# Sums and differences of the MLP token quarters: issued on VectorE instead of GpSimd

## The chip, the cores and the metric

The kernel runs on one core of one Trainium2 chip. The metric is the device time of one execution in microseconds, as the median of several runs. A core has TensorE (PE in the profile, with its weight loads as PEld), VectorE (DVE), ScalarE (ACT), GpSimd (POOL) and a queue that mostly starts DMA transfers (SP). Each takes its instructions in the order in which the built program lists them; they meet through semaphores.

## The reference

One decoder layer on 2048 tokens of width 1024, in float32: a mixing block (retention beside a pooling mixer), a cross-attention into 256 memory tokens, and a gated MLP, each with a root-mean-square norm before it and a residual add behind it. The change touches the MLP alone:

```python
def conv_glu_ffn(h, w_up, conv_w, conv_b, w_down):
    a = h @ w_up
    ...
    c = conv_w[0] * a2 + conv_w[1] * a1 + conv_w[2] * a + conv_b
    gate, val = jnp.split(c, 2, axis=-1)
    return (jax.nn.silu(gate) * val) @ w_down
```

`w_up` is 1024 x 5632 and `w_down` 2816 x 1024; `a1` and `a2` are `a` shifted by one and two tokens.

## The kernel before

Tokens stand along the free axis, in two blocks of 1024 (`b` = 0 and 1) with two halves of 512. A float32 matmul is made of three passes over high and low parts (`passes`, lines 241 to 243), so every operand is first split: ScalarE copies the high part, and VectorE subtracts it to get the low part.

The MLP multiplies with seven products in place of eight (a Strassen scheme). The tokens' matrix and the weights are both seen as 2 x 2 quarters, and each product takes one sum or difference of quarters from each side. The weights' sums are made earlier by DMA (`weight_sums`, lines 918 to 925). The tokens' sums are the subject here. `sums_of` (line 964) takes four 128 x 512 quarters and makes four results in a chain: `t = b22 - b12`, `b12 = b11 - b12`, then `b11 = b11 + t`, `b21 = b11 - b21`. Three of them are written over the quarters. It is called in two places:

- `normed_tiles` makes the inputs of the up projection. For each of four pairs of feature tiles, four quarters come from the DRAM buffer `Xd`, are scaled by the norm (VectorE, line 225, `T<-T,vecs`), three are stored to `Hd`, then come the sums, and four sums are stored to `Hd`. Block 0 does this beside the cross-attention (`first_tiles`), block 1 beside the up projection of block 0 (`later_tiles`). That makes 8 calls.
- `pair` inside `Up.conv` makes the inputs of the down projection. When the gated product of a second feature tile of a pair is done (line 216, `Z<-Z`, 128 x 1024), its two halves are stored to `Gd`, two quarters of the first tile are loaded back from `Gd` into `T`, and the sums follow; they too are stored to `Gd`. With 11 pairs in each of two blocks that makes 22 calls.

So there are 30 calls, with 120 instructions of 128 x 512. The last of the four writes over a quarter that is being stored to `Gd` or `Hd`, and has to wait until that store has been read out.

`combining` loads one sum from `Hd` or `Gd` (line 949), splits it (ScalarE line 956, VectorE line 216 `G<-T,G`), and the result is the right-hand operand of a product. `Member.fetch` loads weights (line 1001), `high` and `low` split them (ScalarE line 1007, VectorE `Q<-R,Q` and `G<-R,G`). `evac` adds or copies a finished product from a PSUM bank into the gate or value tile (VectorE `Z<-Z,mm`). `conv` then runs three taps (ScalarE line 1070, VectorE line 225 `Z<-Z,vecs` of 128 x 1024, twice), SiLU (ScalarE line 1082) and the gated product. GpSimd copies the two tokens at a block's edge into and out of `halo` (lines 1067 and 1069) in `one`.

There are five PSUM banks named `mm`, seven places for split weight pairs and a handful of 128 x 512 temporaries (`T`, and pieces of `consts` and `state`).

The order on each engine is not the order of the source: the kernel is built with `schedule_with_timeline_sim=True`, so that a scheduler orders each engine's instructions by its own estimate of when they can run. Data dependences and buffers are those of the source.

Of the kernel before, what the change touches and what calls it, by code (L numbers as in the profile page):

```python
# [12 lines left out]
ALU = mybir.AluOpType  # L13
# [106 lines left out]
def trunk(ctx, tc, xT, memT, pos, w_qkgu, w_v, wkv, wqT, wo, wout_r, wout_p, poolT, w_up, w_dn, vecs, consts, outT):  # L120
    nc = tc.nc
    pe, act, dve, pool, sp = nc.tensor, nc.scalar, nc.vector, nc.gpsimd, nc.sync
# [64 lines left out]
    t = TT.take()  # L187
# [27 lines left out]
    def tt(eng, out, a, b, op):  # L215
        return eng.tensor_tensor(out=out, in0=a, in1=b, op=op)  # L216
# [746 lines left out]

    def sums_of(b11, b12, b21, b22, t):

        tt(pool, t, b22, b12, ALU.subtract)
        tt(pool, b12, b11, b12, ALU.subtract)
        yield
        tt(pool, b11, b11, t, ALU.add)
        tt(pool, b21, b11, b21, ALU.subtract)  # L970
        yield

    def send(to, aps):
# [53 lines left out]
    class Up(Member):  # L1027
# [29 lines left out]
        def conv(self, g):  # L1057
# [26 lines left out]
            def five():  # L1084
# [15 lines left out]
                def pair():  # L1100
                    if TT.room() < 3:
                        after(1, pair)
                        return
                    x = [TT.take() for _ in range(3)]
                    b11, b12, t = (r.f[:, :SUB] for r in x)
                    sp.dma_start(b12, to[7])
                    sp.dma_start(b11, to[0])
                    todo = sums_of(b11, b12, one, two, t)

                    def keep():  # L1110
                        send(to, {4: t, 1: b12, 2: b11, 6: one})
                        for r in (*x, c):
                            r.free()

                    after(2, lambda: next(todo))
                    after(3, lambda: next(todo))
                    after(5, keep)
# [311 lines left out]
    def normed_tiles(b, j, q, rb):  # L1429

        for i, v in enumerate(q):
            n, s = j + 4 * (i // 2), i % 2
            stt(v, v, ffng[:, n : n + 1], rb[s].f[:, :SUB], ALU.mult, ALU.mult)
        if j == KT // 2 - 1:
            for r in rb:
                r.free()
        yield
        send(Hd[b, j], {0: q[0], 5: q[3], 3: q[2]})
        t = TT.take()
        todo = sums_of(*q, t.f[:, :SUB])  # L1440
        next(todo)
        yield
        next(todo)
        yield
        send(Hd[b, j], {4: t.f[:, :SUB], 1: q[1], 2: q[0], 6: q[2]})
        t.free()
        yield
# [281 lines left out]
```

## Time and profile before

| | |
|---|---|
| median of 3 runs | 2493.02 us (2491.94 to 2494.43) |
| the profiled execution | 2497.84 us |
| its span, first to last instruction | 2495.7 us, mean granted TensorE clock 0.991 |
| PE busy | 2441.3 us (98%), 11390 instructions |
| DVE busy | 1704.0 us (68%), 2789 instructions |
| ACT busy | 1220.2 us (49%), 2171 instructions |
| POOL busy | 374.2 us (15%), 364 instructions |

A row of the timeline or of the groups names the engine, the line, the operation, "output tiles<-input tiles" with buffer numbers left out, and the shape. "[1.2 <-X]" is idle time of that engine ahead of the instruction and what ended it. PEclk is the share of full speed that TensorE was granted. The MLP's part of the span runs from about 1060 us, where block 0's inputs are made beside the cross-attention, to the end.

### The profile page before, as it was taken

What the parts mean: (1) busy time and instruction counts of PE and PEld (TensorE: products, weight loads), DVE (VectorE), ACT (ScalarE), POOL (GpSimd) and SP (SyncE); (2) the same over time, 40 slices, a digit from 0 to 9 for tenths busy, and PEclk for the clock granted to TensorE, in tenths of its full rate; (3) what the DMA queues carried; (4) which work ended last, traced back from release to release, by engine and by line L of the source; (5) the groups of instructions that cost most, each with busy time, mean ns of one, the idle gap of its engine ahead of it and who ended that gap; (6) DMA issues with size and microseconds to landing.
All of it is one profiled execution on the core that took longest, in us unless ns stands there. A gap on an engine that the chain in (4) does not pass through costs nothing. (4 is left out here: it accounts for less than half of the span.)

```text
span 2495.7 us, 33069 instructions
## 1 busy us (share of the span) xinstructions
PE 2441.3 (98%) x11390; PEld 2039.3 (82%) x11390; DVE 1704.0 (68%) x2789; ACT 1220.2 (49%) x2171; POOL 374.2 (15%) x364
## 2 busy tenths in 40 slices
PE   6999999999999999999998999999999999999997
PEld 6888788888788888888887888888888887888885
DVE  8646576564636574575777776896677687877875
ACT  6333423443321223434654555675555576666663
POOL 1010111100111110030025130332113021000001
PEclk9999999999999999999999999999999999999998
DMA  9363889716766764365567565665556468768951
GB/s 317 91 169 110 232 193 244 230 46 208 223 136 151 153 160 152 101 247 199 175 203 250 182 195 158 206 225 172 157 164 214 132 217 300 244 190 282 340 166 68
DMA packets 257176, 474.27 MB, mean 190 GB/s; under 512 B 26864, under 2 KB 56176, under 8 KB 257008
## 3 DMA queue, kind: packets, MB, share of 16 engines
q1 hardware_dynamic: 212336, 408.18, 49.7%
q0 software_dynamic: 19584, 34.61, 9.1%
q10 hardware_dynamic: 25088, 29.37, 3.4%
q8 instruction: 89, 1.46, 0.2%
q14 instruction: 79, 0.65, 0.1%
HBM read 370.87 MB, written 170.39 MB: 217 GB/s over the span
## 5 line engine op out<-in xcount | busy, mean ns | idle before, releaser
L241 PE MATMUL mm<-G,Q 128*128 128x512 f32 (+1 forms) x1888 | 728.3, 386 | 16.1 <-ACT Q L233 10.5
L243 PE MATMUL mm<-G,Q 128*128 128x512 f32 (+1 forms) x1888 | 727.1, 386 | 4.5 <-DVE Q L216 4.5
L242 PE MATMUL mm<-G,Q 128*128 128x512 f32 (+1 forms) x1888 | 726.2, 385 | 0.0
L241 PE MATMUL mm<-G 128*128 128x512 f32 (+1 forms) x1380 | 531.5, 387 | 10.4 <-DVE Z L216 7.3
L243 PE MATMUL mm<-G 128*128 128x512 f32 (+1 forms) x1380 | 532.8, 387 | 2.3 <-DVE G L216 2.3
L242 PE MATMUL mm<-G 128*128 128x512 f32 (+1 forms) x1380 | 533.0, 386 | 0.0
L241 PEld LDWEIGHTS mm<-G,Q 128*128 128x128 f32 x1888 | 358.2, 190 | 84.2 <-ACT Q L233 11.2
L243 PEld LDWEIGHTS mm<-G,Q 128*128 128x128 f32 x1888 | 357.7, 190 | 73.6 <-DVE Q L216 5.4
L242 PEld LDWEIGHTS mm<-G,Q 128*128 128x128 f32 x1888 | 358.3, 190 | 68.0 <-DVE G L216 0.4
L241 PEld LDWEIGHTS mm<-G 128*128 128x128 f32 x1380 | 260.4, 189 | 64.6 <-DVE Z L216 6.3
L243 PEld LDWEIGHTS mm<-G 128*128 128x128 f32 x1380 | 260.6, 189 | 54.6 <-DVE G L216 2.8
L242 PEld LDWEIGHTS mm<-G 128*128 128x128 f32 x1380 | 260.8, 189 | 51.6
L225 DVE SCALAR_TENSOR_TENSOR Z<-Z,vecs 128x1024 f32<-128x1024 f32 x176 | 244.8, 1394 | 55.4 <-ACT Z L1070 50.7
L216 DVE TENSOR_TENSOR Q<-R,Q 128x512 fp32r<-128x512 f32 x235 | 176.0, 751 | 152.2 <-ACT Q L233 142.5
L1007 ACT ACTIVATE G<-R 128x512 fp32r<-128x512 f32 (+1 forms) x272 | 167.1, 615 | 228.7 <-PE mm L242 222.0
L216 DVE TENSOR_TENSOR G<-R,G 128x512 fp32r<-128x512 f32 (+1 forms) x268 | 197.0, 743 | 114.4 <-ACT G L1007 76.0
L216 DVE TENSOR_TENSOR Z<-Z,mm 128x512 f32<-128x512 f32 x284 | 193.6, 682 | 89.3 <-PE mm L243 88.9
L233 ACT ACTIVATE Q<-R 128x512 fp32r<-128x512 f32 x150 | 93.6, 628 | 246.2 <-PE mm L242 219.1
L216 DVE TENSOR_TENSOR G<-T,G 128x512 fp32r<-128x512 f32 (+1 forms) x201 | 135.0, 686 | 51.9 <-ACT G L956 38.4
L1007 ACT ACTIVATE Q<-R 128x512 fp32r<-128x512 f32 (+1 forms) x204 | 125.2, 614 | 76.3 <-PE mm L242 61.9
L1070 ACT ACTIVATE Z<-Z,vecs 128x1024 f32<-128x1024 f32 x88 | 109.3, 1242 | 52.4 <-DVE Z L216 50.8
L941 ACT ACTIVATE aux<-R 128x512 f32<-128x512 f32 (+1 forms) x184 | 105.4, 575 | 47.8 <-DVE Q L216 23.8
(217 smaller groups left out, 2647.7 us busy)
## 6 DMA issues: line engine op xcount, KB each, us to landing
R<-Ud SPq DMA_DIRECT2D x176, 256.0 KB, 2.8
T<-Gd SPq DMA_DIRECT2D x168, 256.0 KB, 4.2
R<-w_up SPq DMA_DIRECT2D x132, 256.0 KB, 3.1
Gd<-Z SPq DMA_DIRECT2D x110, 256.0 KB, 2.5
Ud<-w_up SPq DMA_DIRECT2D x88, 256.0 KB, 6.2
R<-w_qkgu SPq DMA_DIRECT2D x32, 512.0 KB, 4.5
R<-Dd SPq DMA_DIRECT2D x64, 256.0 KB, 4.2
Gd<-T SPq DMA_DIRECT2D x56, 256.0 KB, 3.1
```

Of the source, the lines that this page charges most:

```text
L216: return eng.tensor_tensor(out=out, in0=a, in1=b, op=op)
L225: dve.scalar_tensor_tensor(out=out, in0=a, scalar=s, in1=b, op0=op0, op1=op1)
L233: act.activation(hi, src, AF.Copy)
L241: pe.matmul(ps, lh, rh, start=start, stop=False, skip_group_check=more)
L242: pe.matmul(ps, lh, rl, start=False, stop=False, skip_group_check=more)
L243: pe.matmul(ps, ll, rh, start=False, stop=stop, skip_group_check=more)
L941: act.activation(t, x, AF.Copy)
L1007: act.activation(p2[:, 0, :w], self.raw[i].f[:, :w], AF.Copy)
L1070: act.activation(self.c[g].f, a[:, 2:], AF.Identity, bias=cb[:, f : f + 1], scale=cw[2][:, f : f + 1])
```

## The change

VectorE issues the four instructions of `sums_of`, in both places from which it is called. Nothing else in the source differs; the copies of the block edges and seven multiplications near the end stay on GpSimd.

```diff
     def sums_of(b11, b12, b21, b22, t):
 
-        tt(pool, t, b22, b12, ALU.subtract)
-        tt(pool, b12, b11, b12, ALU.subtract)
-        yield
-        tt(pool, b11, b11, t, ALU.add)
-        tt(pool, b21, b11, b21, ALU.subtract)
+        tt(dve, t, b22, b12, ALU.subtract)
+        tt(dve, b12, b11, b12, ALU.subtract)
+        yield
+        tt(dve, b11, b11, t, ALU.add)
+        tt(dve, b21, b11, b21, ALU.subtract)
         yield
```

Since a scheduler sets the order, the built program differs in more than these 120 instructions. The order of the engines is the same up to the last part of block 1's cross-attention and again in the last part of the down projection; between them PE, VectorE, ScalarE and the SP queue have rows in another order.

## The prediction

> **What bounds the kernel now.** I read the page's first part, then the busy times by stage, PE's waits, the stretches where PE stood, and there the timelines. The span first; the sum is made against the profiled execution of 2497.84 us, 2.1 us more than its span and 4.8 us (0.2%) above the median of the runs, 2493.02. I take the difference from the profile and subtract it from the median.
>
> ```profile
> span 2495.7 us, 33069 instructions
> ```
>
> The busy times by stretch:
>
> ```profile
> core 0: us, PE busy (x) PEld busy (x) DVE busy (x) ACT busy (x) POOL busy (x), PEclk, DMA share, GB/s
> 1626.00:1655.00 29.00, 28.74 (x127) 23.43 (x126) 29.00 (x34) 23.51 (x39) 14.59 (x11) 1.00 0.63 212
> 2045.00:2068.00 23.00, 23.00 (x104) 19.03 (x103) 23.00 (x25) 17.63 (x31) 8.56 (x6) 1.00 0.61 196
> 1352.00:1372.00 20.00, 13.37 (x45) 9.68 (x44) 18.68 (x17) 7.79 (x12) 14.36 (x10) 0.74 0.80 273
> 2070.00:2080.00 10.00, 7.87 (x28) 6.00 (x27) 5.72 (x11) 5.48 (x11) 1.44 (x2) 0.83 1.01 360
> 1376.00:1396.00 20.00, 20.00 (x89) 16.54 (x89) 16.80 (x21) 11.53 (x17) 2.07 (x3) 1.00 0.62 192
> ```
>
> The last row is PE at its pace: 89 matmuls in 20 us, 0.225 us each. TensorE bounds the kernel, and another engine matters only where PE stands. Where the moved instructions run, I find two such places. In 1352 to 1372 there were 45 matmuls, so 44 x 0.225 = 9.9 us were lost, part of it to a clock of 0.74 in these 20 us. In 2070 to 2080 there were 28 where 44.5 fit: 16.5 x 0.225 = 3.7 us. Together 13.6 us, which is all that the change can give back. PE's waits in 1280 to 1420, then in 2030 to 2085, name VectorE both times:
>
> ```profile
> PE mm L241 <- DVE Z L216: 5.2, 2, 4.2
> PE mm L243 <- DVE G L216: 2.3, 1, 2.3
> ```
> ```profile
> PE mm L241 <- DVE Z L216: 2.1, 1, 2.1
> ```
>
> **What the change takes from GpSimd.** Line 216's instructions from 1060 to 2080 us, by engine:
>
> ```profile
> core 0: us, DVE busy (x) POOL busy (x), PEclk, DMA share, GB/s
> 1060.00:2080.00 1020.00, 468.10 (x641) 199.03 (x120) 0.99 0.60 196
> ```
>
> The 120 on POOL are the sums: 199.03 us, 1.66 each. GpSimd bounds nothing, so this by itself is worth nothing. What counts is what they do to VectorE meanwhile. The groups of VectorE from 1200 to 2160 us, which hold 26 of the 30 calls:
>
> ```profile
> L225 DVE SCALAR_TENSOR_TENSOR Z<-Z,vecs 128x1024 f32<-128x1024 f32 x176 | 244.8, 1394 | 55.4 <-ACT Z L1070 50.7 <-issue 2.8 <-DMA R<-Ud 1.1
> L216 DVE TENSOR_TENSOR G<-R,G 128x512 fp32r<-128x512 f32 x142 | 113.4, 799 | 78.0 <-ACT G L1007 75.0 <-DMA Gd<-Z 3.0
> L216 DVE TENSOR_TENSOR Z<-Z,mm 128x512 f32<-128x512 f32 x155 | 105.5, 681 | 25.5 <-PE mm L243 25.2
> L216 DVE TENSOR_TENSOR Q<-R,Q 128x512 fp32r<-128x512 f32 x81 | 67.0, 827 | 8.9 <-ACT Q L1007 8.9
> ```
>
> and the same groups from 1500 to 1585 us, where no sum runs:
>
> ```profile
> L225 DVE SCALAR_TENSOR_TENSOR Z<-Z,vecs 128x1024 f32<-128x1024 f32 x18 | 23.1, 1281 | 7.6 <-ACT Z L1070 7.6
> L216 DVE TENSOR_TENSOR Z<-Z,mm 128x512 f32<-128x512 f32 x14 | 9.6, 683 | 2.0 <-PE mm L243 1.8
> L216 DVE TENSOR_TENSOR G<-R,G 128x512 fp32r<-128x512 f32 x13 | 9.0, 689 | 16.3 <-ACT G L1007 13.3 <-DMA Gd<-Z 3.0
> L216 DVE TENSOR_TENSOR Q<-R,Q 128x512 fp32r<-128x512 f32 x9 | 6.2, 686 | 1.6 <-ACT Q L1007 1.6
> ```
>
> The three groups that read both operands from SBUF are slower in the first table; the one that reads PSUM (`Z<-Z,mm`) is not (681 against 683 ns). So VectorE loses time while GpSimd makes sums: 176 x 0.113 = 19.9 us, 142 x 0.110 = 15.6, 81 x 0.141 = 11.4, together 46.9 us, or 1.8 us for each of 26 calls.
>
> **What it adds to VectorE.** 120 instructions of 128 x 512 with both inputs in SBUF. The timeline of VectorE around the first stall gives their price, and the stall's course:
>
> ```profile
> 1346.52 0.75 DVE L225 SCALAR_TENSOR_TENSOR T<-T,vecs 128x512 f32<-128x512 f32 x1 [5.73 <-DMA T<-Xd]
> ...
> 1349.92 0.75 DVE L225 SCALAR_TENSOR_TENSOR T<-T,vecs 128x512 f32<-128x512 f32 x1 [2.05 <-DMA T<-Xd]
> 1350.59 1.28 DVE L225 SCALAR_TENSOR_TENSOR Z<-Z,vecs 128x1024 f32<-128x1024 f32 x1
> 1351.78 1.78 DVE L216 TENSOR_TENSOR Q<-R,Q 128x512 fp32r<-128x512 f32 x1
> 1353.49 0.68 DVE L216 TENSOR_TENSOR Z<-Z,mm 128x512 f32<-128x512 f32 x1
> 1354.08 1.71 DVE L225 SCALAR_TENSOR_TENSOR Z<-Z,vecs 128x1024 f32<-128x1024 f32 x1
> 1355.72 1.57 DVE L216 TENSOR_TENSOR G<-R,G 128x512 fp32r<-128x512 f32 x1
> 1357.21 2.31 DVE L216 TENSOR_TENSOR Z<-Z 128x1024 f32<-128x1024 f32 x1
> ...
> 1361.43 1.97 DVE L225 SCALAR_TENSOR_TENSOR Z<-Z,vecs 128x1024 f32<-128x1024 f32 x1 [0.23 <-ACT Z L1070]
> 1363.33 0.67 DVE L216 TENSOR_TENSOR Z<-Z,mm 128x512 f32<-128x512 f32 x1
> ```
>
> The instruction at 1353.49 is 0.68 us long, and the next starts 0.59 later: such an instruction holds the engine for 0.60 us. 120 x 0.60 = 72 us in all, 2.4 us for a call. Against the 1.8 us won back, VectorE's load grows by 0.6 us a call, 18 us in 1000 (the smaller groups, which I did not count, would lower this). That is no load that a stage could feel.
>
> The Trainium skill's page "VectorE: DVE Perf Modes", section "The DRAIN you can't avoid", speaks against the change: there the next VectorE instruction does not start until the pipeline is empty. By that rule a sum costs its whole 0.68 us, 82 us in all. The rows with starts 0.59 apart contradict it for instructions that do not depend on each other; inside a call the third and fourth do depend, so the truth may lie between.
>
> **The first stall, 9.9 us.** VectorE stood 5.73 and then 2.05 us for transfers `T<-Xd`, and got behind. From 1349.92 it then worked through its list slowly, since GpSimd ran sums beside it: `Q<-R,Q` took 1.78 in place of 0.69, `G<-R,G` 1.57 in place of 0.69, two `Z<-Z,vecs` 1.71 and 1.97 in place of 1.28: 3.1 us in these four alone. PE waited until the addition `Z<-Z,mm` at 1363.33 was over (1364.0). The transfers were late because the queue that starts them stood for sums on GpSimd; its timeline (one merged row for three stores of sums, 4.72 us, and the load behind them):
>
> ```profile
> 1337.22 4.72 SPq L975 DMA_DIRECT2D Gd<-T  x3
> ...
> 1342.52 0.40 SPq L1453 DMA_DIRECT2D T<-Xd  x1
> ```
>
> A call lasts 4 x 1.66 = 6.6 us on GpSimd and some 2.4 us, plus what is put between, on VectorE, so these stores, and the loads behind them, come earlier. In the changed kernel's order, between the last of the two scalings at 1349.92 and that `Z<-Z,mm` stand one product addition, one `G<-R,G` and two sums: 0.67 + 4 x 0.60 + 0.68 = 3.75 us, done at 1353.7 in place of 1364.0 even if the transfer lands no earlier. I take the whole 9.9 us as gone. If the cover fails (the sums wait there too), 3.1 us remains as the gain.
>
> **The second stall, 3.7 us.** ScalarE, then VectorE:
>
> ```profile
> 2071.81 0.63 ACT L956 ACTIVATE G<-T 128x512 fp32r<-128x512 f32 x1 [7.34 <-DMA T<-Gd]
> ```
> ```profile
> 2072.47 0.69 DVE L216 TENSOR_TENSOR G<-T,G 128x512 fp32r<-128x512 f32 x1 [3.77 <-ACT G L956]
> 2073.08 0.68 DVE L216 TENSOR_TENSOR Z<-Z,mm 128x512 f32<-128x512 f32 x1
> ```
>
> VectorE waited for a late load of a sum, and the addition that PE needed was queued behind. In the changed order that addition stands ahead of these `G<-T,G`. But PE needs the late operand too, soon after. Between 0 and 3.7 I take half, 1.9.
>
> **The new wait.** The fourth instruction of a call overwrites a quarter that is being stored. The page's row for that store:
>
> ```profile
> Gd<-Z SPq DMA_DIRECT2D x110, 256.0 KB, 2.5
> ```
>
> On GpSimd nobody stood behind this wait but the copies of the block edges; on VectorE the additions that free PE's banks do, and the low parts of weights. The closest place in the new order has two other instructions and three sums between the gated product and the fourth: 5 x 0.60 = 3.0 us against 2.5 and the issue, so a wait of some tenths. The bounds for all calls: nothing, or one stall like the first, 9.9. I take 2, since most gaps are wider. The edge copies, no longer queued behind 6.6 us of sums, cost nothing and can only come earlier. The 16 sums beside the cross-attention add 9.6 us to VectorE there; no PE wait on VectorE is seen in it, five PSUM banks cover it, and I take nothing (at most 9.6).
>
> **Sum:** -9.9 - 1.9 + 2 = -9.8 us. Profiled execution 2497.84 - 9.8 = 2488.0; median 2493.02 - 9.8 = 2483.2, so 2483. What a measurement of this kernel can tell from no change is about 0.2%, 5 us: faster is below 2488, slower above 2498.
>
> **Rivals.** *The transfers alone made the stalls.* For it: 5.73 + 2.05 us of standing ahead of the first one, and a load ahead of the second; and VectorE's load does not shrink. Then only the 3.1 us are won, 2490: no change that can be told. Against it: the new order has less between load and addition.
>
> *VectorE, waiting in order, starves PE.* Place: 1626 to 1655 and 2045 to 2068, where the table shows VectorE busy without a gap and two calls close together. Eight sums and two waits for stores, 8 x 0.60 + 2 x 2.5 = 9.8 us, could stand ahead of the additions. The first stall shows from where it decides: PE stood after VectorE had stood 7.8 us and lost 3.1, 10.9 in all. If it happens once, at the price of the seen stall, and the old ones stay: 2493 + 9.9 = 2503. Against it: GpSimd's sums take 1.8 us a call from VectorE in these places now, and PE lost next to nothing in them.
>
> *The change doesn't do what it says:* excluded, the built program has 120 more instructions on VectorE and 120 fewer on GpSimd.
>
> **Chances.** Forecast, both stalls mostly gone: 0.55. No change: 0.18. Slower: 0.27; the schedule between 1060 and 2170 us is a new one, and any wait in it lands on an engine that was hardly ever late. The range: at the lower end all 13.6 us, 2479, and a microsecond for the runs' spread, 2478; at the upper end 2500, which leaves out the worse half of the slower case.
>
> **What would show it.** Right: POOL busy near 175 us; `G<-R,G` and `Q<-R,Q` at 0.69 throughout; PE's waits on VectorE in 1280 to 1420 under 2 us and no slice with a low PEclk there. Wrong: a new PE wait on `Z L216` or `G L216` with VectorE standing ahead of it for a DMA into or out of `Gd`, `Hd` or `Xd`; or `T<-T` on VectorE well over 0.7 us.

## The result, and the profile after

The changed kernel takes 2477.96 us (median of 6 runs, 2475.03 to 2482.13) where the kernel before took 2493.01 on the same chip (6 runs, 2490.11 to 2495.33). The ratio is 0.9944, with a 95% interval of 0.9934 to 0.9954: 15.05 us or 0.6% faster. Its profiled execution took 2477.89 us.

The page of the changed kernel, its span, its busy times and the store that the fourth sum of a call waits for:

```profile
span 2476.1 us, 33012 instructions
...
PE 2434.1 (98%) x11390; PEld 2034.9 (82%) x11390; DVE 1707.3 (69%) x2909; ACT 1219.5 (49%) x2171; POOL 187.3 (8%) x244
...
Gd<-Z SPq DMA_DIRECT2D x110, 256.0 KB, 2.7
```

VectorE executes 120 instructions more and is busy only 3.3 us longer (1704.0 before). Where the 15 us were lost is counted best in matmuls. These are the busy times by stretches of 100 us of the kernel before, in the columns that the prediction's table has:

```profile
1300.00:1400.00 100.00, 92.41 (x392) 74.88 (x391) 78.95 (x85) 49.44 (x75) 45.36 (x31) 0.95 0.73 244
1600.00:1700.00 100.00, 99.74 (x440) 82.28 (x439) 87.44 (x104) 69.15 (x113) 33.45 (x25) 1.00 0.69 226
2000.00:2100.00 100.00, 97.87 (x425) 80.57 (x424) 82.10 (x107) 71.83 (x134) 28.52 (x19) 0.98 0.76 253
```

and of the changed kernel:

```profile
1300.00:1400.00 100.00, 100.00 (x443) 82.81 (x442) 85.98 (x115) 54.00 (x83) 9.32 (x11) 1.00 0.75 251
1600.00:1700.00 100.00, 100.00 (x443) 82.81 (x442) 83.32 (x108) 64.73 (x99) 16.17 (x16) 1.00 0.59 197
2000.00:2100.00 100.00, 99.67 (x440) 82.19 (x439) 85.12 (x133) 76.89 (x145) 0.19 (x1) 1.00 0.85 286
```

PE at its pace makes 443 in 100 us, so one takes 0.2257 us. The three stretches hold 51, 3 and 15 matmuls more: 11.5, 0.7 and 3.4 us, together 15.6, about the 15.05 between the medians. (The two profiled executions lie 19.6 us apart in span. The other 4 us lie ahead of 1100 us, mostly in 200 to 300 us, where the order of the engines is the same in both kernels and the profiled execution before, 4.8 us above its median, was slow: no gain of the change.) In the first stretch PEclk goes from 0.95 to 1.00, and in all three VectorE has room: it makes 30 instructions more in the first one at 86% busy.

VectorE's wait for the loads `T<-Xd` in 1280 to 1480 us, around the first stall, is halved; the kernel before, then the changed one (us in total, times, longest):

```profile
DVE T L225 <- DMA T<-Xd: 11.2, 4, 5.7
```
```profile
DVE T L225 <- DMA T<-Xd: 5.6, 4, 3.4
```

In 1060 to 2160 us PE waits for VectorE's additions once in the changed kernel (7.3 us in all before):

```profile
PE mm L241 <- DVE Z L216: 0.3, 1, 0.3
```

The groups of VectorE in 1200 to 2160 us, and the sums themselves (last row, of 1060 to 2160 us):

```profile
L225 DVE SCALAR_TENSOR_TENSOR Z<-Z,vecs 128x1024 f32<-128x1024 f32 x176 | 224.7, 1280 | 50.1 <-ACT Z L1070 45.2 <-issue 2.8 <-DMA state<-Gd 1.1
L216 DVE TENSOR_TENSOR Z<-Z,mm 128x512 f32<-128x512 f32 x161 | 109.7, 682 | 39.9 <-PE mm L243 39.7
L216 DVE TENSOR_TENSOR G<-R,G 128x512 fp32r<-128x512 f32 x145 | 99.3, 687 | 72.3 <-ACT G L1007 69.0 <-DMA R<-Ud 3.3
L216 DVE TENSOR_TENSOR Q<-R,Q 128x512 fp32r<-128x512 f32 x81 | 55.6, 686 | 13.9 <-ACT Q L1007 13.7
...
L216 DVE TENSOR_TENSOR T<-T 128x512 f32<-128x512 f32 x71 | 48.7, 686 | 4.7 <-ACT T L356 4.0
```

1394, 799 and 827 ns have become 1280, 687 and 686, and `Z<-Z,mm` stays (681, now 682). A sum takes 0.69 us where GpSimd took 1.66.

### The profile page after: what moved, and what is told of

Same layout as the page of the kernel before. It is cut to its first block, busy times and chain, and to the rows that moved or that the text cites. A ratio compares the mean times of both kernels' runs of the same rounds, so it can differ in the third digit from the quotient of the medians.

```text
span 2476.1 us, 33012 instructions
## 1 busy us (share of the span) xinstructions
PE 2434.1 (98%) x11390; PEld 2034.9 (82%) x11390; DVE 1707.3 (69%) x2909; ACT 1219.5 (49%) x2171; POOL 187.3 (8%) x244
## 4 chain that ended last, share of the span: by engine, by line
PE 94%; DVE 2%; DMA 2%; ACT 1%; issue 1%; POOL 0%; SPq 0%; POOLq 0%; ACTq 0%; DVEq 0%
PE mm L241 30%; PE mm L243 29%; PE mm L242 29%; DVE Z L216 1%; PE aux L750 1%; PE aux L851 1%; PE aux L763 1%; PE aux L243 1%; PE aux L241 1%; PE aux L242 1%; PE aux L739 1%; PE aux L765 1%; DMA VWd<-T 0%; DVE G L216 0%; DVE Q L216 0%
## 5 line engine op out<-in xcount | busy, mean ns | idle before, releaser
L241 PEld LDWEIGHTS mm<-G,Q 128*128 128x128 f32 x1888 | 358.0, 190 | 85.2 <-ACT Q L233 11.4
L216 DVE TENSOR_TENSOR Q<-R,Q 128x512 fp32r<-128x512 f32 x235 | 162.6, 694 | 155.1 <-ACT Q L233 140.7
L225 DVE SCALAR_TENSOR_TENSOR Z<-Z,vecs 128x1024 f32<-128x1024 f32 x176 | 224.7, 1280 | 50.1 <-ACT Z L1070 45.2
L216 DVE TENSOR_TENSOR G<-R,G 128x512 fp32r<-128x512 f32 (+1 forms) x268 | 178.8, 675 | 110.4 <-ACT G L1007 70.7
L216 DVE TENSOR_TENSOR T<-T 128x512 f32<-128x512 f32 (+3 forms) x218 | 149.1, 689 | 15.6 <-ACT T L356 8.0
```

Of the source, the lines that this page charges most:

```text
L225: dve.scalar_tensor_tensor(out=out, in0=a, scalar=s, in1=b, op0=op0, op1=op1)
L241: pe.matmul(ps, lh, rh, start=start, stop=False, skip_group_check=more)
```

## The experiments

Three explanations were to be told apart. **A, company:** two-input instructions of VectorE are slowed while GpSimd sums beside them, and so free PE's banks late. **Rival 1, held loads:** sums that are ready late on GpSimd hold stores, and the loads behind them, so that VectorE stands. **B, order:** the scheduler arranged the rest differently once the sums were on another engine. The edits are against the changed kernel unless another one is named. The runs were made on several chips, on which the kernel before took 2491.11 to 2495.45 us. Ratios are to the kernel before beside the run, and runs from different chips are compared by what each wins against it; the changed kernel wins 15.05 us.

**1. The same order for both.** Both kernels were built in program order, so that TensorE's order is the same in the two but for six rows:

```diff
-    with tile.TileContext(nc, schedule_with_timeline_sim=True) as tc:
+    with tile.TileContext(nc, schedule_with_timeline_sim=False) as tc:
```

Sums on GpSimd:

> The sums on GpSimd, as before, but built without the scheduler's time estimate (schedule_with_timeline_sim=False), so that the order of the engines changes little when the sums move. This is the base for its partner, which has the sums on VectorE; its own time is not forecast beyond being slower than 2493 us, since the estimate no longer helps. Theory A (GpSimd's sums slow VectorE down and hold up the SP queue): this one is at least 10 us slower than its partner, and its groups G<-R,G and Q<-R,Q lie over 0.75 us. Rival B (the gain came from the scheduler's new order alone): the two lie within 5 us of each other.

Sums on VectorE:

> The sums on VectorE, built without the scheduler's time estimate; in its list, TensorE's order is that of its partner but for 6 rows. Theory A: at least 10 us faster than its partner, with G<-R,G and Q<-R,Q at 0.69 us. Rival B: within 5 us of it.

Measured: 2515.07 us on GpSimd (ratio to the kernel before 1.0081, 1.0065 to 1.0098) and 2489.26 on VectorE (0.998, 0.997 to 0.999). The stretch of the first stall with the sums on GpSimd, then on VectorE:

```profile
1300.00:1400.00 100.00, 87.59 (x356) 70.30 (x355) 75.94 (x77) 46.28 (x69) 37.03 (x28) 0.93 0.66 216
```
```profile
1300.00:1400.00 100.00, 99.42 (x439) 82.01 (x438) 82.93 (x110) 56.34 (x84) 3.44 (x10) 1.00 0.73 243
```

`G<-R,G` and `Q<-R,Q` take 780 and 814 ns in 1200 to 2160 us with the sums on GpSimd, 686 and 688 on VectorE, as expected. With hardly any difference in TensorE's order the sums' place is worth 25.8 us, more than under the scheduler. So a new order of TensorE (B) is not what makes the gain. PE's waits in 1060 to 2160 us with the sums on GpSimd:

```profile
PE mm L241 <- ACT Z L1053: 11.3, 5, 3.8
PE mm L241 <- ACT G L956: 6.6, 1, 6.6
```

Here PE waits for ScalarE and not for VectorE. The first of these waits lies at the first stall, where ScalarE itself stood 11.7 us for VectorE's taps (`Z L225`, 1290 to 1410 us; 2.1 us in the partner): VectorE's lateness reaches PE through another engine. The second lies at 2087 us, behind 5.9 us in which ScalarE stood for a load `T<-Gd` of a sum. The engine that a wait names is the last link only.

**2. Company without held loads.** The sums stay on VectorE, and GpSimd gets work that nothing of the kernel reads, beside 26 calls; 208 additions of 128 x 256 on a constant:

```diff
         tt(dve, t, b22, b12, ALU.subtract)
+        if scr:
+            pool.tensor_copy(scr[0][:, :1], t[:, :1])
+            for _ in range(8):
+                tt(pool, scr[0].rearrange("p (o b) -> p o b", o=2), wide, wide, ALU.add)
         tt(dve, b12, b11, b12, ALU.subtract)
...
```

> The changed kernel, with GpSimd given as much to do beside each of the 26 calls that run during the up projection: after the first difference is made, one 128 x 1 copy and 8 additions of 128 x 256 that read a constant and write 512 bytes that nobody reads. VectorE makes the sums as in the changed kernel, and no store waits for GpSimd. Theory A1 (the slowdown of VectorE while GpSimd reads SBUF is what made PE stand): G<-R,G and Q<-R,Q rise to about 0.8 us again, VectorE loses some 47 us or more, and PE's stalls come back, 2486 to 2500 us. Theory A2 (it was the length of a call on GpSimd, 6.6 us, which held the stores and loads up): no PE wait comes back, 2478 us within 5. Rival B (order): 2478 within 5 as well.

Measured: 2488.97 us (0.9979, 0.9969 to 0.999), 10.0 us less won than by the changed kernel. The stretch, that of the second place, and VectorE's waits for those loads and for GpSimd in 1280 to 1480 us:

```profile
1300.00:1400.00 100.00, 95.75 (x413) 78.02 (x412) 92.23 (x108) 50.61 (x77) 60.96 (x67) 0.98 0.74 246
2000.00:2100.00 100.00, 97.88 (x427) 79.60 (x426) 89.80 (x125) 73.00 (x135) 32.73 (x39) 1.00 0.77 255
```
```profile
DVE T L225 <- DMA T<-Xd: 2.4, 3, 1.6
DVE T L225 <- POOL T L216: 1.9, 1, 1.9
```

In the first stretch 30 matmuls or 6.8 us are lost, and VectorE stands no longer for loads than in the changed kernel; one wait of 1.9 us is for the added work itself, and with it VectorE still stands less (4.3 us against 5.6). The second place has 13 matmuls fewer than in the changed kernel. The added work by GpSimd's groups, and VectorE's groups in 1200 to 2160 us:

```profile
L216 POOL TENSOR_TENSOR T<-consts 128x256 bf16<-128x256 f32 x208 | 197.7, 950 | 14.9
```
```profile
L225 DVE SCALAR_TENSOR_TENSOR Z<-Z,vecs 128x1024 f32<-128x1024 f32 x176 | 229.1, 1305 | 47.1 <-ACT Z L1077 43.8 <-issue 3.2
L216 DVE TENSOR_TENSOR Z<-Z,mm 128x512 f32<-128x512 f32 x157 | 106.8, 680 | 30.5 <-PE mm L243 30.4
L216 DVE TENSOR_TENSOR G<-R,G 128x512 fp32r<-128x512 f32 x143 | 100.7, 706 | 65.2 <-ACT G L1014 64.7 <-PE mm L242 0.5
L216 DVE TENSOR_TENSOR Q<-R,Q 128x512 fp32r<-128x512 f32 x82 | 62.3, 760 | 12.1 <-ACT Q L1014 8.5 <-PE mm L242 3.4
```

The groups that read SBUF twice grow (1280 to 1305, 687 to 706, 686 to 760), the one that reads PSUM does not. They grow less than was expected: 0.8 us and 47 us or more of VectorE's time were named, and `G<-R,G` is at 0.71, with VectorE busy 38.5 us longer in all (1745.8 against 1707.3). The time came out as expected all the same, since a stall is made in one place, and a mean over 960 us does not show it. In VectorE's timeline at the first stall single instructions are 0.41 us longer:

```profile
1342.86 1.10 DVE L216 TENSOR_TENSOR Q<-R,Q 128x512 fp32r<-128x512 f32 x1
1343.88 1.10 DVE L216 TENSOR_TENSOR Z<-T,Z 128x512 f32<-128x512 f32 x1
```

Company alone makes a stall. GpSimd is busier here than in the kernel before (60.96 against 45.36 us in the stretch), and this profiled execution was the longest of the ten, so 6.8 is at the high end for it.

**3. Length alone.** The first sum is issued five times over, so that VectorE has 120 instructions more, and GpSimd none:

```diff
-        tt(dve, t, b22, b12, ALU.subtract)
+        for _ in range(5):
+            tt(dve, t, b22, b12, ALU.subtract)
```

> The changed kernel with the first of the four instructions issued five times (the same result each time), so that a call has 8 instructions on VectorE and its load grows by 120 x 0.60 = 72 us more, with no GpSimd beside it. If VectorE has room and only bursts of slowdown or late transfers hurt (theory A), the time stays within 5 us of 2478. If VectorE's load in the dense places decides (the rival of the prediction in which VectorE starves PE), PE stands at the turn of the blocks near 1640 us and before the down projection near 2060 us, and the time is 2488 us or more.

Measured: 2485.31 us (0.9963, 0.995 to 0.9975), 6.4 us less won than by the changed kernel, between what the two theories expected. The stretches:

```profile
1300.00:1400.00 100.00, 100.00 (x443) 82.81 (x442) 92.87 (x128) 54.39 (x83) 11.26 (x10) 1.00 0.74 239
1600.00:1700.00 100.00, 100.00 (x443) 82.81 (x442) 91.26 (x123) 67.03 (x105) 12.35 (x16) 1.00 0.66 211
2000.00:2100.00 100.00, 95.72 (x406) 77.51 (x406) 85.46 (x134) 72.88 (x138) 0.50 (x2) 0.97 0.77 254
```

72 us more of VectorE's work cost PE nothing in the stretches from 1000 to 2000 us, at up to 93% busy. The price is paid in one place, 34 matmuls fewer than in the changed kernel or 7.7 us in 2000 to 2100, where the last sums of the up projection are stored and loaded again as the first operands of the down projection.

**4. One half of the change each.** `sums_of` takes its engine as an argument, and only one of the two callers gets VectorE.

```diff
-    def sums_of(b11, b12, b21, b22, t):
+    def sums_of(b11, b12, b21, b22, t, eng):
...
-                    todo = sums_of(b11, b12, one, two, t)
+                    todo = sums_of(b11, b12, one, two, t, dve)
...
-        todo = sums_of(*q, t.f[:, :SUB])
+        todo = sums_of(*q, t.f[:, :SUB], pool)
```

> Only the sums of the gated products (22 calls of 4, for the down projection) are made by VectorE; those of the normalised tokens (8 calls) stay on GpSimd. The first stall, 1340 to 1372 us, lies among the calls for the tokens of the second block, the second stall (2070 us) behind a call for a gated product. Theory A (VectorE is slowed wherever GpSimd sums beside it, and each call counts where PE is short of cover): the first stall stays in part, 4 to 11 us lost between 1300 and 1400, with GpSimd still busy over 20 us there; the second goes; time 2484 to 2489. Rival C (only the sums of the gated products matter, since they are 88 of 120): both stalls go, 2478 to 2481. Theory A has G<-R,G between 0.69 and 0.75 as a mean of 1200 to 2160 us, with the slow ones beside the token calls alone.

With `pool` and `dve` changed about:

> The other half: only the 8 calls for the normalised tokens are on VectorE, the 22 for the gated products stay on GpSimd. Theory A: the first stall goes for the larger part (3 us or less lost between 1300 and 1400), the second (2070 us, 3 to 4 us) stays; 2481 to 2486. Rival C: little changes, 2488 to 2493. If both halves together win clearly less than the 15 us of the whole change, each leaves something that the other needs (the two kinds of call lie close to one another at the first stall).

Measured: 2483.48 us with the 22 calls of `pair` on VectorE (0.9967, 0.9955 to 0.9979), 2486.01 with the 8 calls of `normed_tiles` (0.998, 0.9971 to 0.9989), the kernel before 2491.11 beside them. That is 7.6 and 5.1 us won, 12.7 together, which the intervals cannot tell from the whole change. The 8 calls are worth two thirds of the 22, so the place of a call counts, and not the number of calls alone. The first stall of the one and of the other, with VectorE's wait for `T<-Xd` in 1280 to 1480 us:

```profile
1300.00:1400.00 100.00, 97.91 (x427) 79.50 (x426) 83.94 (x97) 52.75 (x81) 26.32 (x22) 1.00 0.69 235
```
```profile
DVE T L225 <- DMA T<-Xd: 7.1, 5, 2.7
```
```profile
1300.00:1400.00 100.00, 97.03 (x418) 78.98 (x417) 82.12 (x101) 52.21 (x81) 23.48 (x18) 0.98 0.74 250
```
```profile
DVE T L225 <- DMA T<-Xd: 11.5, 5, 4.8
```

The first half comes close to what company had it do (company of the token sums stays): 16 matmuls or 3.6 us are lost where 4 or more were expected, and the time is half a microsecond under the range. The second half does not go as expected. In the first stall it loses 5.6 us and not 3 or less, and in the second place, where 3 to 4 us were to stay, it makes 435 matmuls, 5 or 1.1 us fewer than the changed kernel. GpSimd's timeline with the token sums on VectorE shows its last sum of a `pair` call and then an edge copy, with nothing between:

```profile
1338.06 1.29 POOL L216 TENSOR_TENSOR Z<-T,Z 128x512 f32<-128x512 f32 x1
1353.58 2.92 POOL L1069 COPY halo<-Z 128x2 f32<-128x2 f32 x1 [14.22 <-DVE Z L216]
```

PE stands most between 1350 and 1360 us, with 25 matmuls where 44 fit. No sum runs on GpSimd beside that stall, and yet 25 matmuls or 5.6 us of the stretch are lost, behind loads that are as late as before (11.5 against 11.2 us). Held loads therefore have a part of their own.

**5. Held loads without company.** Two, then six, one-column pieces are loaded ahead of the first tile of a token call of the second block, one after the other, so that the load comes late and its queue stands.

```diff
-            sp.dma_start(r.f[:, :SUB], Xd[b, j + 4 * (i // 2)][:, i % 2 * SUB : (i % 2 + 1) * SUB])
+            [sp.dma_start(r.f[:, :1], Xd[b, j][:, h : h + 1]) for h in range(6) if b and not i]; sp.dma_start(r.f[:, :SUB], Xd[b, j + 4 * (i // 2)][:, i % 2 * SUB : (i % 2 + 1) * SUB])
```

Two pieces, in program order and under the scheduler:

> The changed kernel in program order (that of the run with sums on VectorE whose emission does not follow a timeline), TensorE's order the same as there, and in addition the loads T<-Xd of the four token calls of the second block are held: into the first of a call's four tiles two one-column pieces are loaded one after the other before the tile itself, so that the tile comes some 4 us or more later and the queue that starts loads and stores stands as long. No sum is on GpSimd. It costs the disputed transfers by themselves. Theory A (VectorE's slowness beside GpSimd is the larger part, the held transfers the smaller): VectorE's wait for T<-Xd rises from 8 us to over 15, and PE loses 0 to 4 us against 2489.3: 2489 to 2493. Rival 1 (the late transfers alone make PE's stalls): it loses 7 us or more, 2496 or more, with a new PE wait on VectorE or ScalarE behind them between 1290 and 1400.

> The same held loads in the changed kernel itself, where the order of emission follows a timeline and so moves other loads and, in some rows after 1290 us, TensorE's matmuls about. Theory A: 0 to 4 us more than the changed kernel, 2477 to 2482. Rival 1: 7 us or more, 2485 or more, lost between 1290 and 1400.

Measured: 2485.66 us (0.9966, 0.9953 to 0.998) and 2478.97 (0.9937, 0.9917 to 0.9958), no loss in either. But VectorE's wait did not grow (2.8 and 5.2 us), against what was expected: the hold fell into cover, and these two runs decide nothing. Six pieces:

> The held loads again, three times as long: six one-column pieces ahead of the first tile of each token call of the second block, in the changed kernel. With two pieces VectorE had stood 5.2 us for T<-Xd between 1280 and 1480 us (5.6 in the changed kernel, 11.2 in the one before), so the hold had mostly fallen into cover and tested little. With six, some 12 to 15 us each, VectorE should stand 11 us or more there, as in the kernel before. Theory A (GpSimd's company is the larger part of the stall): 0 to 5 us lost against the changed kernel, 2477 to 2483. Rival 1 (the late transfers alone): as in the kernel before, 9 us or more lost in 1300 to 1400, 2486 or more.

> Six pieces in program order, with TensorE's order that of the other two runs in program order. VectorE stood 7.9 us for T<-Xd between 1280 and 1480 with the sums on GpSimd, 3.4 with them on VectorE, 2.8 with two pieces. Theory A: VectorE's wait at or above 7.9 us, PE loses 0 to 5 us against 2486 to 2489, so 2486 to 2494. Rival 1: PE loses 10 us or more, as with the sums on GpSimd (12 us in 1300 to 1400), 2498 or more.

Measured: 2486.77 us under the scheduler (0.9964, 0.9951 to 0.9976), 6.4 us less won than by the changed kernel, and 2490.63 in program order (0.9985, 0.9976 to 0.9995), where as much is won as without the pieces (4.8 us). In program order VectorE's wait stayed at 2.3 us, so that run decides nothing either. Under the scheduler it rose to that of the kernel before:

```profile
1300.00:1400.00 100.00, 95.90 (x413) 78.89 (x412) 80.37 (x106) 50.10 (x78) 7.22 (x10) 0.97 0.75 244
```
```profile
DVE T L225 <- DMA T<-Xd: 13.0, 7, 4.2
```
```profile
PE mm L241 <- DVE Z L216: 4.1, 1, 4.1
```

VectorE stands 13.0 us, runs at its quiet pace afterwards, and PE loses 30 matmuls, 6.8 us, with the very wait that the kernel before had. Held loads alone make a stall too; theory A, in which they were the small part, falls. Rival 1, by which they are all of it and 9 us or more go in this stretch, is not fully met either.

**6. Company with the loads' queue freed.** In the kernel before, GpSimd starts the stores of the sums itself, so that the queue of the loads never stands for a sum:

```diff
-            sp.dma_start(to[i], a)
+            (q or sp).dma_start(to[i], a)
...
-                        send(to, {4: t, 1: b12, 2: b11, 6: one})
+                        send(to, {4: t, 1: b12, 2: b11, 6: one}, pool)
...
-        send(Hd[b, j], {4: t.f[:, :SUB], 1: q[1], 2: q[0], 6: q[2]})
+        send(Hd[b, j], {4: t.f[:, :SUB], 1: q[1], 2: q[0], 6: q[2]}, pool)
```

> The kernel before, with the sums on GpSimd, but the four stores that follow each call's sums are started by GpSimd's own queue, so that the queue of the loads (SP) never stands for a sum. It leaves GpSimd's company as it is and takes away the held loads: the reverse of the run with six held pieces (12.4 us of SP's standing for GpSimd's sums go by each 250 us). With either cause alone 6.6 to 6.8 us had been lost at the first stall, with both 11.45. Theory D (two causes, each enough for a stall of its own): SP's waits on POOL fall from 72 us to under 5, VectorE's wait for T<-Xd in 1280 to 1480 from 11.2 to under 7, G<-R,G stays at 0.78 or more, and 3 to 7 us are won: 2486 to 2490 where the kernel before has 2493. Theory A (company alone): 2491 or more. Rival 1 (held loads alone): all of the first stall goes, 2478 to 2483. What GpSimd needs to start 120 stores (0.8 us each by its other transfers) lengthens its calls and could cost some us in all three.

(The figure in its bracket is wrong: the queue's waits on GpSimd add up to 75.9 us in 1060 to 2100, about 18 in 250.) Measured: 2499.39 us (1.0028, 1.0016 to 1.004), slower than the kernel before, against all three theories. The queue's waits for GpSimd went (75.9 to 1.2 us), but what it aimed at did not, and the first stall stayed: 399 matmuls, 44 or 9.9 us fewer than the changed kernel. VectorE's wait for `T<-Xd` in 1280 to 1480, then the queue's own waits in 1330 to 1372:

```profile
DVE T L225 <- DMA T<-Xd: 14.6, 5, 6.2
```
```profile
SPq L1453 <- DMA Gd<-T: 4.0, 2, 3.1
```

The load now waits for its tile: `T` comes free when the last sums of a `pair` call have been stored, and those end only when GpSimd is through. So a long call makes loads late through its tiles too, whichever queue starts its stores; the 4.0 us are what is seen of it here, and what the rest of the 14.6 us is due to was not followed up. The run cannot say what company costs without held loads; the second one does. And there is a new loss of 31 matmuls against 450 in 1100 to 1200 us, among the token sums beside the cross-attention, where GpSimd now starts their stores too. PE waits there for VectorE's scaling `T<-T,sm` (line 220), of which the last section has the durations:

```profile
PE aux L851 <- DVE T L220: 3.6, 2, 2.6
```
```profile
1100.00:1200.00 100.00, 96.36 (x419) 79.05 (x418) 55.80 (x88) 41.99 (x79) 10.35 (x15) 0.97 0.68 229
```

**7. Further in the same direction.** Five sums of squares of the memory's norm, once in the first 100 us, also on VectorE:

```diff
-                tt(pool, f[:, :SUB], f[:, :SUB], f[:, SUB:], ALU.add)
+                tt(dve, f[:, :SUB], f[:, :SUB], f[:, SUB:], ALU.add)
...
```

> The changed kernel, and the five sums of squares of the memory's norm (once, in the first 30 us) on VectorE too: five instructions, 5 to 6 us less on GpSimd, 2.5 to 3 us more on VectorE. Theory A: VectorE's instructions there keep their quiet duration, but PE in the first 100 us waits mostly for loads, so 0 to 3 us are won: 2475 to 2478, no difference that can be told. Rival: VectorE, which has the split of the first weights to make then, is the one that is late at the start: 2 to 4 us lost, 2480 to 2482.

Measured: 2479.23 us (0.9957, 0.9944 to 0.9971), which lies between the two expected ranges and cannot be told from the changed kernel (0.9944, 0.9934 to 0.9954). No version beat the changed kernel.

**What follows.** At the first stall the kernel before had both causes and lost 51 matmuls; held loads alone 30 (and 25 in the half), company alone 30, neither none. Each of the two is enough for a stall of some 5 to 7 us, and together they cost less than their sum. (Each count is of one profiled execution.) The change takes both away at once: four sums take some 2.4 us of VectorE's time and no longer 6.6 of GpSimd's, and GpSimd no longer sums beside VectorE. At the second place company alone lost 13 matmuls, nearly the 15 of the kernel before; the half that left the 22 calls on GpSimd lost 5, and held loads alone were not tried there. So how its 3.4 us divide stays open.

## Why the prediction was right, and where it was off

The direction and the mechanism held; forecast 2483, measured 2477.96, which is 0.04 us outside the stated range's lower end. The gain is 15.05 us where 9.8 were forecast. That the result lies at the edge and not well outside is luck: the lower end was the 13.6 us, taken as the most that could be won, and one microsecond. By its steps:

- **What the change can give back, 13.6 us:** too small, as 15.6 us were given back. The first stall was sized on 1352 to 1372 alone (9.9 us); the stretch of 100 us has 11.5, since PE had already stood a little before 1352 (1 us in 1330 to 1352). And 0.7 us in 1600 to 1700 lay in a place taken as intact.
- **VectorE's time, 46.9 us won back:** right. The three groups shrank by 20.1 us, 145 x 0.112 = 16.2 and 11.4, together 47.7. The net growth, 18 us, was too high: VectorE is busy 3.3 us longer in all. The smaller groups that were left out won too, such as the scalings beside the cross-attention, below.
- **A sum holds VectorE 0.60 us, or 0.68 by the rule of the Trainium skill's page "VectorE: DVE Perf Modes", section "The DRAIN you can't avoid":** the prediction left out that the same section lets a next instruction that is not held back start earlier, so that the rows 0.59 us apart do not contradict the page. "The truth may lie between" is nearly what the timeline of the changed kernel shows:

```profile
1335.54 0.68 DVE L216 TENSOR_TENSOR T<-T 128x512 f32<-128x512 f32 x1
1336.26 0.69 DVE L216 TENSOR_TENSOR Z<-T,Z 128x512 f32<-128x512 f32 x1
...
1341.27 0.69 DVE L216 TENSOR_TENSOR G<-R,G 128x512 fp32r<-128x512 f32 x1
1341.87 1.22 DVE L216 TENSOR_TENSOR Z<-Z 128x1024 f32<-128x1024 f32 x1
```

  Of two sums of one call that depend on each other the second starts 0.72 us after the first; instructions that do not depend on each other start 0.60 apart. By either the load was no matter, which the third experiment shows with as much again up to 2000 us.
- **First stall, all gone:** right, and its two parts, the slow list and the late loads, were both named. The 3.75 us forecast from the second scaling to the end of the product addition came true: 1343.01 to 1346.75 us in the changed kernel's timeline, with the four instructions in between that were named. What failed was how they were weighed: 3.1 us for the slow instructions if the transfers stayed late, and "no change" for the rival of the transfers. The runs give 6.8 us to either cause alone.
- **"The transfers were late because the queue that starts them stood for sums":** incomplete. With that queue freed they were no earlier (VectorE stood 14.6 us for them, 11.2 before), and part of it is the tiles that the sums keep.
- **Second stall, half:** too cautious, 3.4 of 3.7 us went.
- **The new wait, +2 us:** it did not come under the scheduler. The store takes 2.7 us, VectorE's waits for stores to `Gd` and `Hd` are 0.2 us in 1060 to 2160 us, and PE's waits on VectorE's additions 0.3. In program order it did come: VectorE's sums stood 5.7 us for `Gd<-Z` and 1.4 for `Hd<-T` (in the calls for the tokens the third sum, too, writes over a quarter that is being stored), and PE still made 439 of 443 matmuls at the first stall. So the wait is real, the scheduler's order hides it, and it is cheap. This and the second stall are most of what the forecast lacked; the rest is the first stall's size and the 0.7 us above.
- **Edge copies and the 16 sums beside the cross-attention, nothing:** right; no PE wait on VectorE is seen in 1060 to 1200 us.
- **What was to be seen:** the groups at 0.69 and no low PEclk came true. POOL shows 187.3 us and not 175, as its 88 edge copies have become longer (493 and 609 ns before, in the order of the rows):

```profile
L1067 POOL COPY Z<-halo 128x2 f32<-128x2 f32 x44 | 30.0, 682 | 367.8 <-DVE Z L225 367.8
L1069 POOL COPY halo<-Z 128x2 f32<-128x2 f32 x44 | 29.5, 670 | 429.8 <-DVE Z L216 429.8
```

Of the rival in which VectorE starves PE the third experiment shows what it would have taken: with the sums' load doubled, VectorE still kept up in 1600 to 1700, and lost 7.7 us only where the down projection begins.

## What to carry to other kernels

Work on an idle engine is not free if it makes a busy neighbour's instructions longer: compare the mean duration of the same group where the neighbour works and where it does not, and see whether the operands' places (SBUF or PSUM) tell the slow groups from the others. The length of a helper's chain counts as much, since its stores, the tiles that it keeps and the loads into them all wait for its end; a faster engine can shorten all of it though it is the busier one. A stall with two causes does not go by halves: take each away alone before its price is put down to one of them.

## What the runs showed of the hardware that was not expected

The slowing goes both ways. The edge copy of 128 x 2 in the last GpSimd timeline above took 2.92 us (1353.58 to 1356.50) beside four two-input instructions that VectorE ran without a gap (1353.42 to 1356.45); the same copy took 0.19 us at 1340.15 in the kernel before.

And it is not confined to two inputs. VectorE's scaling with one tensor input, `T<-T,sm` of 128 x 256, beside the cross-attention: the kernel before, the one whose GpSimd also starts stores, and the one with the token sums on VectorE, by groups in 1060 to 1200 us:

```profile
L220 DVE TENSOR_SCALAR T<-T,sm 128x256 f32<-128x256 f32 x18 | 11.0, 651 | 0.4
```
```profile
L220 DVE TENSOR_SCALAR T<-T,sm 128x256 f32<-128x256 f32 x18 | 13.4, 785 | 0.5
```
```profile
L220 DVE TENSOR_SCALAR T<-T,sm 128x256 f32<-128x256 f32 x16 | 4.9, 349 | 0.1
```

These numbers look like whole instructions waiting for whole instructions: 0.69 us grows by up to 0.41 beside additions of 0.95 us, and by 1.09 (to 1.78) beside sums that take 1.29 us themselves when nothing delays them (1338.06 above). The Trainium skill's page "SBUF — State Buffer" says in its section "SBUF: two separate sides" that VectorE and GpSimd share a pair of ports as "an exclusive lock, not a bandwidth split": a GpSimd instruction holds it, or a VectorE instruction in a two-port mode, or a VectorE instruction with two SBUF inputs, this last only against a GpSimd instruction that reads SBUF. The rows agree in which two-input groups are slowed, in both directions, and in the sizes on VectorE's side. The copy was held for longer than any one VectorE instruction beside it (1.23 us at most), so it must have waited for several. That a lock is the mechanism no run here shows by itself, nor that the scaling ran in a two-port mode.
